# Small triangular inverses moved from two engines to one, and a softplus written with fewer operations, in a two-layer hybrid encoder

## The chip, the cores and the metric

The kernel runs on one core of a Trainium2 chip. The metric is the time of one execution on the device, in microseconds (us); the number to beat is the median of three runs. The profile is of one more execution. The engines are named as the profile names them: PE is TensorE's matrix products, PEld its weight loads, DVE is VectorE, ACT ScalarE, POOL GpSimd, SP SyncE, which here only issues DMAs.

## The reference

Two layers of an encoder over 256 tokens of 1024 channels, in float32. In each layer one projection of the normalised input feeds two token mixers, retention and a gated delta rule in both directions, and two gates. The delta rule is done in chunks of 128 tokens, 8 heads, and needs two things that matter here: a decay g from a softplus, and the inverse of a unit triangular matrix of 128 x 128 for each chunk, head and direction.

```python
h = rmsnorm(x, norm1_g[l])
(r_q, r_k, r_v, r_g, d_q, d_k, d_v, d_z, d_b, d_a, gate_raw) = split_cols(h @ w_in[l])
o = retention_bidir(rotary(r_q), rotary(r_k), r_v)           # then group norm, silu(r_g)
qkv = silu(centred_dwconv(concat([d_q, d_k, d_v]), conv_w[l]))   # 5 taps
beta = sigmoid(d_b)
g = -exp(a_log[l]) * softplus(d_a + dt_bias[l])
od = gated_delta_chunked(...) forward + the same on the flipped sequence
x = x + (gA * (y_ret @ w_proj_ret[l]) + gB * (y_dn @ w_proj_dn[l])) @ w_out[l]
x = x + square(relu(rmsnorm(x) @ w_ff1[l])) @ w_ff2[l]

# inside gated_delta_chunked, per chunk:
gc = cumsum(g)
a_mat = beta[..., :, None] * (kc @ kc.T) * exp(gc_i - gc_j) below the diagonal
sol = triangular_solve(a_mat + eye(CHUNK), rhs, lower=True, unit_diagonal=True)
```

## The kernel before

**Weights and products.** Every weight streams in once, in chunks of 512 KB, by DMAs that SP issues (lines L187 and L205; the tiles are wraw and wrawc, three buffers). ACT copies a chunk to a rounded tile whi (L177), and DVE subtracts that from the original to get the rest, wlo (L178); so a float32 product becomes three products with 32-bit rounded operands. whi and wlo have three buffers each. tok_chunk (L194 to L196) makes 12 products of 512 columns from a chunk, chan_pair (L212 to L214) 24 products of 256 columns. Loads and splits are given a priority that puts them 45 steps ahead of their products (WPRI).

**A layer** has these parts, in the order of the code. Norm 1 and the transposed input. Then gates_small: a small projection, softplus on it (L283 to L308), the product with triangles of ones for the cumulative decays (ps_gc, L313), their rows to DRAM (rowd, L326) and back, spread over all partitions, as E (L333). POOL subtracts the columns (L336) and keeps one triangle (L340), ACT takes the exponential. Then retention and the delta rule, interleaved; then the gates and output projections (chan_pair over ga, pr, gb, pd), and the feed-forward part, which is long and streams weights only.

**The delta rule** is a generator with these steps, for two halves of four heads each:

- half_inputs: for each pair of heads conv_pair, that is chan_pair, then DVE puts the result in a padded tile (xpad, L363), ACT makes tap 0 into an accumulator cacc (L369), POOL tap 4 into cac for the first 16 heads (L371) and ACT for the others, DVE adds taps 1 to 3 (three operations, L375), POOL adds cac to cacc (L376). ACT then makes Silu of it (kq, L394), and TensorE transposes it (ps_kt, L396).
- delta_kk: products of keys and queries (ps_kk), multiplied on DVE with E. The 32 x 32 diagonal blocks of the triangular matrix A go to DRAM (gd).
- delta_solve, once for both halves: the 128 diagonal blocks come back as one block per partition (Gm, L478, 128 x 1024), and the inverse of each is solved there into X, by rows. Step j subtracts the product of row j of A with column j of X from the part of X right of j; there are 30 steps. A step is a pair of operations: a product into stm (L487) and a subtraction in X (L489). X is first set to -Gm (L481), and its diagonal to 1 (L482). The columns of the inverse do not depend on each other, so two engines share them: DVE solves four, POOL the other 28.
- delta_levels: a transposed copy XT (L491, DVE), both to DRAM (xd L493, xtd L494), and back by 40 small DMAs into the tiles dd, D64 and DT of the two halves; then products build the inverses of blocks of 64 (ps_y, L528; ps_m, L538; ps_mt) and of 128 (ps_y6, ps_m6).
- half_v: the same convolution for the values, Silu (L430) in place, and its transposes (ps_vt, L432); delta_out: the recurrence itself.

The parts of the solve that the change touches:

```python
CV = 4
...
for e, c0, c1 in ((V, 0, CV), (G, CV, 32)):
    e.tensor_scalar(X[:, c0:c1, :], Gm[:, c0:c1, :], -1.0, None, ALU.mult)     # L481
    e.memset(X.rearrange("p a b -> p (a b)")[:, 33 * c0:33 * c1 - 32:33], 1.0)
    for j in range(c0 + 1, 31):
        n, w = 31 - j, min(j, c1) - c0
        ...                      # stm = Gm row j x X column j (L487), X -= stm (L489)
```

**The order.** Retention (0) and the delta rule (1) are interleaved by steps in the order `SEQ = "11111011101101"`. That is the order of the code; a scheduler that simulates the engines with costs of its own then sets the order of the instructions on each engine, with the priorities given. An engine runs its instructions in that order, one after the other; so does SP its DMA issues. An instruction whose input is late holds up all that stand behind it on the same engine. The retention part that lies beside the solve consists of its tok_chunks, its scores (ps_st, L690, times a mask into sT, L692) and outputs (ps_ro, L697).

Of the kernel before, what the change touches and what calls it, by code (L numbers as in the profile page):

```python
# [8 lines left out]
F32 = mybir.dt.float32  # L9
F32R = mybir.dt.float32r  # L10
AF = mybir.ActivationFunctionType
ALU = mybir.AluOpType
AX = mybir.AxisListType

P = 128
# [20 lines left out]
def tile_trunk(ctx, tc, x, norm1_g, w_in, conv_w, a_log, dt_bias, ret_gn_g, dn_norm_g,  # L36
# [18 lines left out]
    # how far ahead of the products their weights are loaded and split  # L55
    WPRI = 45
    WRAW = 3
    # the order of the steps of retention (0) and of the delta rule (1)
    SEQ = "11111011101101"
    # columns of the 32 x 32 inverses that VectorE solves; GpSimd the others  # L60
    CV = 4
    # heads whose last tap of the convolution is GpSimd's
    PT = 16
# [31 lines left out]
    def upper(t, s):  # L95
        """keeps t[p, j] where s (j - p) >= 0"""
        G.affine_select(t, t, pattern=[[s, P]], base=0, channel_multiplier=-s, compare_op=ALU.is_ge, fill=0.0)
# [28 lines left out]
    def parameters():  # L126
        # triangles of ones: i <= j, i >= j
        G.memset(tri, 1.0)
        upper(trif, 1)
        upper(trib, -1)  # L130
        columns(cw[0], crow[0], CK * 24)
        A.activation(nega, nega, AF.Exp)
        V.tensor_scalar(nega, nega, -1.0, None, ALU.mult)
# [10 lines left out]
    def rms(nm, xh):  # L144
        """1 / rms of each token: [P, NT]"""
# [11 lines left out]
    def tsplit(src, scale, dst_hi, dst_lo, nm):  # L157
        """dst[j][:, k, :] (channels on partitions) = scale * src transposed, as a float32r pair"""
# [22 lines left out]
    def tok_chunk(w, hi, lo, nk, nm):  # L181
        """two banks [tokens, 512] = act @ w (nk k-tiles of 128 rows, 512 columns)"""
# [16 lines left out]
    def chan_pair(w, hi, lo, nm):  # L199
        """two banks [128 columns of w, S tokens] for w of 256 columns"""  # L200
# [20 lines left out]
    for l in range(DEPTH):  # L221
# [32 lines left out]
        def gates_small():  # L254
# [12 lines left out]
            with tc.high_priority(offset=300):  # L267
# [14 lines left out]
                # softplus(a + dt) = max(a, 0) + log1p(exp(-|a|))  # L282
                ad = s16("ad")  # L283
                G.tensor_tensor(ad, ab[:, :, 16:32],
                                dtb[:, 16 * l:16 * l + 16].unsqueeze(1).broadcast_to([P, NT, 16]), ALU.add)
                m = s16("spm")
                G.tensor_scalar(m, ad, 0.0, None, ALU.max)
                G.tensor_tensor(y, ad, m, ALU.subtract)
                G.tensor_tensor(y, y, m, ALU.subtract)
                A.activation(by, by, AF.Exp)  # L290
                # beta = 1 / (1 + exp(-b)); z = y / (2 + y)
                z = s16("spz")
                V.tensor_scalar(z, y, 2.0, None, ALU.add)
                V.reciprocal(z, z)
                V.tensor_scalar(beta, beta, 1.0, None, ALU.add)
                V.reciprocal(beta, beta)
                G.tensor_tensor(z, z, y, ALU.mult)
                w2 = s16("spw")
                G.tensor_tensor(w2, z, z, ALU.mult)
                p = s16("spp")  # L300
                G.tensor_scalar(p, w2, 1.0 / 15.0, None, ALU.mult)
                for n in (13, 11, 9, 7, 5, 3, 1):
                    G.tensor_scalar(p, p, 1.0 / n, None, ALU.add)
                    G.tensor_tensor(p, p, w2 if n > 1 else z, ALU.mult)
                G.tensor_scalar(p, p, 2.0, None, ALU.mult)
                G.tensor_tensor(p, p, m, ALU.add)
                g = s16("gg")
                G.tensor_tensor(g, p, nega[:, 16 * l:16 * l + 16].unsqueeze(1).broadcast_to([P, NT, 16]), ALU.mult)  # L308
                # cumulative decays of each chunk, both ways
# [17 lines left out]
            # decays of each pair of tokens, exp(gc_i - gc_j) where i is past j and zero elsewhere  # L327
# [28 lines left out]
        def conv_pair(off, cwoff):  # L356
            """two heads (256 columns): silu(conv(proj)) with channels on partitions, unsilu'd accumulators"""
# [85 lines left out]
        # direction, first and second block of the pairs of blocks that make a block of 64  # L443
        PAIRS = ((0, 0, 1), (0, 2, 3), (1, 1, 0), (1, 3, 2))

        def delta_kk(hf, q):
            """decays, A and attn of a half; the 32 x 32 diagonal blocks of A to DRAM"""
# [27 lines left out]
        def delta_solve():  # L475
            """inverses of the 32 x 32 diagonal blocks, one block per partition"""
# [3 lines left out]
            for e, c0, c1 in ((V, 0, CV), (G, CV, 32)):  # L480
                e.tensor_scalar(X[:, c0:c1, :], Gm[:, c0:c1, :], -1.0, None, ALU.mult)  # L481
                e.memset(X.rearrange("p a b -> p (a b)")[:, 33 * c0:33 * c1 - 32:33], 1.0)  # L482
                for j in range(c0 + 1, 31):
                    n, w = 31 - j, min(j, c1) - c0
                    tm = sm.tile([P, 256 if c0 else 128], F32, tag=f"stm{c0}", name="stm", bufs=1)
                    tv = tm[:, :w * n].rearrange("p (a b) -> p a b", a=w)
                    e.tensor_tensor(tv, Gm[:, j, j + 1:].unsqueeze(1).broadcast_to([P, w, n]),  # L487
                                    X[:, c0:c0 + w, j:j + 1].broadcast_to([P, w, n]), ALU.mult)
                    e.tensor_tensor(X[:, c0:c0 + w, j + 1:], X[:, c0:c0 + w, j + 1:], tv, ALU.subtract)  # L489
# [7 lines left out]
        def delta_levels(hf, q):  # L497
            """transposed inverses of the whole chunks' I + A"""
# [4 lines left out]
            Dv = (xtv, xv)     # rows of D of each direction  # L503
            DTv = (xv, xtv)    # rows of its transpose
# [7 lines left out]
            for b in range(4):  # L512
                # as the first block of a pair, and as the second one
# [11 lines left out]
            # blocks of 64: the pairs of both directions at once  # L525
# [27 lines left out]
            # blocks of 128  # L553
# [373 lines left out]
```

## Time and profile before

| | us |
|---|---|
| three runs | 1134.62, 1137.21, 1139.95 |
| median | 1137.21 |
| span of the profiled execution | 1132.0 |
| TensorE busy in it | 1081.0 (95%) |
| DVE busy | 794.1 (70%) |
| ACT busy | 588.2 (52%) |
| POOL busy | 375.5 (33%) |

The profiled execution is one of its own, whose time is known by its span alone: from the first to the last instruction on the engines, without what the launch adds around it. A line of the profile's windows gives a stretch of time and how long each engine was busy in it; a line of its waits gives an instruction's engine, tile and line, what it waited for, and for how long in all, how often, and at most. A line of the timeline gives start, duration, engine, line and operation, with the output and inputs by the names above, and in square brackets how long the engine had been idle before and who released it. "PEclk" is the clock that TensorE was granted, 1.00 being full speed.

### The profile page before, as it was taken

The page shows a single profiled execution, that of the slowest core. Times are in us where ns is not written, and L with a number is a line of the kernel's source. Part 1 is how long each engine was busy: PE and PEld are TensorE (multiplying, and loading weights), DVE is VectorE, ACT ScalarE, POOL GpSimd, SP SyncE. Part 2 cuts the span into 40 slices and gives each one's busy share as a digit, 9 for nine tenths or more (in the row PEclk, how much of TensorE's full clock was granted, in tenths as well). Part 3 has the DMA queues.
Part 4 walks back from the last instruction along what each step waited for, and adds up shares of the span by engine and source line. Part 5 has one row for each costly group of instructions (what it writes and reads, how often), then busy time and mean ns, then how long its engine had stood idle before and what let it go on. Part 6 is the DMA issues. An engine that isn't in the chain of part 4 may idle for free.

```text
span 1132.0 us, 19926 instructions
## 1 busy us (share of the span) xinstructions
PE 1081.0 (95%) x7572; PEld 999.6 (88%) x7572; DVE 794.1 (70%) x1354; ACT 588.2 (52%) x1012; POOL 375.5 (33%) x431
## 2 busy tenths in 40 slices
PE   7979989899999999999998799899999999999997
PEld 6979877799999899988898798778999999999885
DVE  5889989556766666645478999895657676666453
ACT  5677644343355565544367675444334556655342
POOL 4888486100002043300069972940001011332000
PEclk9999999999999999999999999999999999999999
DMA  7464663543465566556564556455443565655653
GB/s 231 150 181 140 180 189 120 132 149 97 130 185 186 168 192 183 185 190 208 175 203 142 174 158 198 135 165 121 128 139 115 176 212 165 201 181 181 199 188 110
DMA packets 175762, 188.45 MB, mean 166 GB/s; under 512 B 36240, under 2 KB 137010, under 8 KB 175666
## 3 DMA queue, kind: packets, MB, share of 16 engines
q1 hardware_dynamic: 174288, 185.17, 53.1%
q10 hardware_dynamic: 1378, 2.02, 0.6%
q8 instruction: 59, 0.97, 0.4%
q14 instruction: 37, 0.30, 0.1%
HBM read 181.85 MB, written 5.31 MB: 165 GB/s over the span
## 4 chain that ended last, share of the span: by engine, by line
PE 70%; DVE 12%; POOL 7%; DMA 3%; issue 3%; SPq 2%; ACT 2%; POOLq 0%; DVEq 0%; ACTq 0%
PE pcf L212 5%; PE pcf L213 5%; PE pcf L214 5%; PE paf L195 5%; PE paf L196 5%; PE paf L194 5%; DVE wlo L178 4%; DVE cacc L375 2%; POOL cacc L376 1%; POOL X L489 1%; PE pcgb L214 1%; PE pcgb L212 1%; PE pcgb L213 1%; DMA wrawc<-in_w_in_dram 1%; PE pawo L196 1%
## 5 line engine op out<-in xcount | busy, mean ns | idle before, releaser
L178 DVE TENSOR_TENSOR wlo<-wrawc,whi 128x1024 fp32r<-128x1024 f32 x192 | 244.4, 1274 | 119.6 <-ACT whi L177 118.5
L177 ACT ACTIVATE whi<-wrawc 128x1024 fp32r<-128x1024 f32 x192 | 202.4, 1055 | 158.9 <-PE pcpr L213 29.0
L178 DVE TENSOR_TENSOR wlo<-wraw,whi 128x1024 fp32r<-128x1024 f32 x128 | 158.7, 1241 | 101.2 <-ACT whi L177 101.0
L177 ACT ACTIVATE whi<-wraw 128x1024 fp32r<-128x1024 f32 x128 | 135.4, 1058 | 132.7 <-PE paf L196 85.6
L213 PE MATMUL pcf<-h2l,whi 128*128 128x256 f32 x512 | 143.7, 283 | 0.0
L214 PE MATMUL pcf<-h2h,wlo 128*128 128x256 f32 x512 | 143.0, 283 | 0.0
L212 PE MATMUL pcf<-h2h,whi 128*128 128x256 f32 x512 | 142.0, 284 | 0.0
L214 PE MATMUL pcd<-hTh,wlo 128*128 128x256 f32 x384 | 109.6, 292 | 2.4 <-DVE wlo L178 2.4
L212 PE MATMUL pcd<-hTh,whi 128*128 128x256 f32 x384 | 111.1, 293 | 0.4 <-DVE xpad L363 0.2
L213 PE MATMUL pcd<-hTl,whi 128*128 128x256 f32 x384 | 110.7, 290 | 0.0
L848 POOL TENSOR_TENSOR fz<-fz 128x256 f32<-128x256 f32 x64 | 66.1, 1034 | 118.1 <-ACT fz L847 117.1
L195 PE MATMUL paf<-wlo,fh 128*128 128x512 f32 x256 | 100.3, 392 | 0.0
L196 PE MATMUL paf<-whi,fl 128*128 128x512 f32 x256 | 100.0, 391 | 0.0
L213 PEld LDWEIGHTS pcf<-h2l,whi 128*128 128x128 f32 x512 | 98.2, 192 | 0.0
L214 PEld LDWEIGHTS pcf<-h2h,wlo 128*128 128x128 f32 x512 | 98.0, 192 | 0.0
L212 PEld LDWEIGHTS pcf<-h2h,whi 128*128 128x128 f32 x512 | 97.1, 192 | 0.0
L194 PE MATMUL paf<-whi,fh 128*128 128x512 f32 x256 | 89.6, 389 | 0.0
L375 DVE SCALAR_TENSOR_TENSOR cacc<-xpad,cw,cacc 128x256 f32<-128x256 f32 x144 | 83.6, 603 | 5.8 <-ACT cacc L369 5.5
L214 PEld LDWEIGHTS pcd<-hTh,wlo 128*128 128x128 f32 x384 | 73.9, 195 | 3.1 <-DVE wlo L178 2.6
L212 PEld LDWEIGHTS pcd<-hTh,whi 128*128 128x128 f32 x384 | 74.9, 196 | 1.8 <-DVE rw L665 0.6
L213 PEld LDWEIGHTS pcd<-hTl,whi 128*128 128x128 f32 x384 | 75.0, 195 | 0.7 <-issue 0.2
L141 POOL TENSOR_TENSOR odf<-sso,mh 128x8 f32<-128x8 f32 x4 | 6.5, 1637 | 199.6 <-DVE sso L642 199.6
(279 smaller groups left out, 2841.2 us busy)
## 6 DMA issues: line engine op xcount, KB each, us to landing
wrawc<-in_w_in_dram SPq DMA_DIRECT2D x96, 512.0 KB, 3.9
wrawc<-in_w_ff_dram SPq DMA_DIRECT2D x64, 512.0 KB, 3.6
wraw<-in_w_ff_dram SPq DMA_DIRECT2D x64, 512.0 KB, 3.6
wraw<-in_w_in_dram SPq DMA_DIRECT2D x48, 512.0 KB, 3.5
wrawc<-in_w_proj_ret_dram SPq DMA_DIRECT2D x16, 512.0 KB, 3.4
wrawc<-in_w_proj_dn_dram SPq DMA_DIRECT2D x16, 512.0 KB, 3.9
wraw<-in_w_out_dram SPq DMA_DIRECT2D x16, 512.0 KB, 3.7
E<-rowd SPq DMA_DIRECT2D x16, 256.0 KB, 5.8
```

Of the source, the lines that this page charges most:

```text
L177: A.activation(hv, raw, AF.Copy)
L178: V.tensor_tensor(lv, raw, hv.bitcast(F32), ALU.subtract)
L194: T.matmul(ps[t], lhsT=a, rhs=wh[:, kk, :], start=k == 0, stop=False)
L195: T.matmul(ps[t], lhsT=a, rhs=wl[:, kk, :], start=False, stop=False)
L196: T.matmul(ps[t], lhsT=b, rhs=wh[:, kk, :], start=False, stop=k == nk - 1)
L212: T.matmul(ps[i], lhsT=wh[:, kk, c], rhs=a, start=k == 0, stop=False)
L213: T.matmul(ps[i], lhsT=wh[:, kk, c], rhs=b, start=False, stop=False)
L214: T.matmul(ps[i], lhsT=wl[:, kk, c], rhs=a, start=False, stop=k == KT - 1)
L375: V.scalar_tensor_tensor(a, xp[:, k:k + S], wk(k), a, ALU.mult, ALU.add)
L376: G.tensor_tensor(a, a, b, ALU.add)
L489: e.tensor_tensor(X[:, c0:c0 + w, j + 1:], X[:, c0:c0 + w, j + 1:], tv, ALU.subtract)
L848: G.tensor_tensor(z2, z, z, ALU.mult)
```

## The change

It does two things. The solve runs on DVE alone: one negation, one memset of the diagonal, and one pair of operations per step j over all j columns that are not finished, so 30 pairs. And softplus, which was 20 operations on POOL beside a few on DVE and ACT, runs on DVE in 14 more: a multiplication and an addition are joined in one operation each time (scalar_tensor_tensor). The series has the same terms as before. Comments and descriptions are dropped as well, so that line numbers after are two to four lower.

```diff
-                G.tensor_tensor(ad, ab[:, :, 16:32],
+                V.tensor_tensor(ad, ab[:, :, 16:32],
                                 dtb[:, 16 * l:16 * l + 16].unsqueeze(1).broadcast_to([P, NT, 16]), ALU.add)
                 m = s16("spm")
-                G.tensor_scalar(m, ad, 0.0, None, ALU.max)
-                G.tensor_tensor(y, ad, m, ALU.subtract)
-                G.tensor_tensor(y, y, m, ALU.subtract)
+                V.tensor_scalar(m, ad, 0.0, None, ALU.max)
+                V.scalar_tensor_tensor(y, m, -2.0, ad, ALU.mult, ALU.add)
                 A.activation(by, by, AF.Exp)
                 z = s16("spz")
                 V.tensor_scalar(z, y, 2.0, None, ALU.add)
                 V.reciprocal(z, z)
+                V.tensor_tensor(z, z, y, ALU.mult)
+                w2 = s16("spw")
+                V.tensor_tensor(w2, z, z, ALU.mult)
+                p = s16("spp")
+                V.tensor_scalar(p, w2, 1.0 / 15.0, None, ALU.mult)
+                for n in (13, 11, 9, 7, 5, 3):
+                    V.scalar_tensor_tensor(p, p, 1.0 / n, w2, ALU.add, ALU.mult)
+                V.scalar_tensor_tensor(p, p, 1.0, z, ALU.add, ALU.mult)
+                V.scalar_tensor_tensor(p, p, 2.0, m, ALU.mult, ALU.add)
+                g = s16("gg")
+                V.tensor_tensor(g, p, nega[...], ALU.mult)
                 V.tensor_scalar(beta, beta, 1.0, None, ALU.add)
                 V.reciprocal(beta, beta)
-                G.tensor_tensor(z, z, y, ALU.mult)
-                w2 = s16("spw")
-                G.tensor_tensor(w2, z, z, ALU.mult)
-                p = s16("spp")
-                G.tensor_scalar(p, w2, 1.0 / 15.0, None, ALU.mult)
-                for n in (13, 11, 9, 7, 5, 3, 1):
-                    G.tensor_scalar(p, p, 1.0 / n, None, ALU.add)
-                    G.tensor_tensor(p, p, w2 if n > 1 else z, ALU.mult)
-                G.tensor_scalar(p, p, 2.0, None, ALU.mult)
-                G.tensor_tensor(p, p, m, ALU.add)
-                g = s16("gg")
-                G.tensor_tensor(g, p, nega[...], ALU.mult)
...
-            for e, c0, c1 in ((V, 0, CV), (G, CV, 32)):
-                e.tensor_scalar(X[:, c0:c1, :], Gm[:, c0:c1, :], -1.0, None, ALU.mult)
-                e.memset(X.rearrange("p a b -> p (a b)")[:, 33 * c0:33 * c1 - 32:33], 1.0)
-                for j in range(c0 + 1, 31):
-                    n, w = 31 - j, min(j, c1) - c0
-                    tm = sm.tile([P, 256 if c0 else 128], F32, tag=f"stm{c0}", name="stm", bufs=1)
-                    tv = tm[:, :w * n].rearrange("p (a b) -> p a b", a=w)
-                    e.tensor_tensor(tv, Gm[:, j, j + 1:].unsqueeze(1).broadcast_to([P, w, n]),
-                                    X[:, c0:c0 + w, j:j + 1].broadcast_to([P, w, n]), ALU.mult)
-                    e.tensor_tensor(X[:, c0:c0 + w, j + 1:], X[:, c0:c0 + w, j + 1:], tv, ALU.subtract)
+            V.tensor_scalar(X, Gm, -1.0, None, ALU.mult)
+            V.memset(X.rearrange("p a b -> p (a b)")[:, 0:1024:33], 1.0)
+            for j in range(1, 31):
+                n = 31 - j
+                tm = sm.tile([P, 256], F32, tag="stm", name="stm", bufs=1)
+                tv = tm[:, :j * n].rearrange("p (a b) -> p a b", a=j)
+                V.tensor_tensor(tv, Gm[:, j, j + 1:].unsqueeze(1).broadcast_to([P, j, n]),
+                                X[:, :j, j:j + 1].broadcast_to([P, j, n]), ALU.mult)
+                V.tensor_tensor(X[:, :j, j + 1:], X[:, :j, j + 1:], tv, ALU.subtract)
```

The scheduler sets the instructions of the changed kernel in another order in three places that matter.

POOL, from the last convolution add ahead of the solve in layer 0 (each row is a line, an operation, its output, its inputs and the shape). Before:

```order
L376 TENSOR_TENSOR cacc<-cacc,cac_2175 128x256
L481 TENSOR_SCALAR X<-Gm 128x896
L376 TENSOR_TENSOR cacc<-cacc,cac_2184 128x256
L482 MEMSET X 128x28
L487 TENSOR_TENSOR stm<-Gm,X 128x26
L489 TENSOR_TENSOR X<-X,stm 128x26
L487 TENSOR_TENSOR stm<-Gm,X 128x50
L489 TENSOR_TENSOR X<-X,stm 128x2x25
```

After:

```order
L468 COPY W<-A_1329 32x8x32 x2
L468 COPY W<-A_1330 32x8x32 x2
L373 TENSOR_TENSOR cacc<-cacc,cac_2086 128x256
L373 TENSOR_TENSOR cacc<-cacc,cac_2095 128x256
L373 TENSOR_TENSOR cacc<-cacc,cac_2253 128x256
L373 TENSOR_TENSOR cacc<-cacc,cac_2262 128x256
```

Two by two, the convolution adds of the values follow each other on POOL now (L373 is L376 of before), and the 52 solve steps that stood between them are gone from this queue.

SP, from the load of Gm to the first small DMA of the levels (dd) in layer 0. Before:

```order
L478 DMA Gm<-gd 128x1024
L187 DMA wraw<-in_w_in_dram 128x2x512 x4
L205 DMA wrawc<-in_w_in_dram 128x4x256 x2
L187 DMA wraw<-in_w_in_dram 128x2x512 x8
L205 DMA wrawc<-in_w_in_dram 128x4x256 x2
L493 DMA xd<-X 128x1024
L494 DMA xtd<-XT 128x1024
L205 DMA wrawc<-in_w_in_dram 128x4x256
L515 DMA dd<-xd 32x8x32
```

After:

```order
L475 DMA Gm<-gd 128x1024
L185 DMA wraw<-in_w_in_dram 128x2x512 x2
L203 DMA wrawc<-in_w_in_dram 128x4x256 x2
L185 DMA wraw<-in_w_in_dram 128x2x512 x8
L203 DMA wrawc<-in_w_in_dram 128x4x256 x6
L489 DMA xd<-X 128x1024
L203 DMA wrawc<-in_w_in_dram 128x4x256
L490 DMA xtd<-XT 128x1024
L511 DMA dd<-xd 32x8x32
```

Between the blocks' load and xd stand 18 weight loads now, and 16 before; Gm itself stands two loads later, so xd follows 58 loads of the layer and not 54.

TensorE, at the second half's first level in layer 0. Before, gate products (pcga) and transposes of retention's output (pstyr) stand between ps_y, ps_m and what follows:

```order
L214 MATMUL pcga_3058<-hTh_124,wlo 128x256
L528 MATMUL ps_y<-dd,W 128x32 x8
L538 MATMUL ps_m<-W,DT_1572 32x32 x8
L164 MATMUL pstyr<-ident,rg_2658 128x128 x8
L212 MATMUL pcga_3058<-hTh_124,whi 128x256
```

After:

```order
L212 MATMUL pcga_3167<-hTh_123,wlo 128x256
L524 MATMUL ps_y<-dd,W 128x32 x8
L534 MATMUL ps_m<-W,DT_1483 32x32 x8
L534 MATMUL ps_m<-W,DT_1484 32x32 x8
L534 MATMUL ps_m<-W,DT_1509 32x32 x8
L534 MATMUL ps_m<-W,DT_1510 32x32 x8
L541 MATMUL ps_mt<-dd,W 128x32 x16
L210 MATMUL pcga_3166<-hTh_124,whi 128x256
```

The levels of 64 of both halves stand together now, with no other products among them.

More of the change, by code (lines that the diff above doesn't have):

```diff
@@ L59, in tile_trunk @@
     SEQ = "11111011101101"
-    CV = 4
     PT = 16
@@ L294, in gates_small @@
                 V.reciprocal(z, z)
+                V.tensor_tensor(z, z, y, ALU.mult)
[8 more added lines that the diff above has]
+                g = s16("gg")
+                V.tensor_tensor(g, p, nega[:, 16 * l:16 * l + 16].unsqueeze(1).broadcast_to([P, NT, 16]), ALU.mult)
                 V.tensor_scalar(beta, beta, 1.0, None, ALU.add)
                 V.reciprocal(beta, beta)
-                G.tensor_tensor(z, z, y, ALU.mult)
-                w2 = s16("spw")
-                G.tensor_tensor(w2, z, z, ALU.mult)
-                p = s16("spp")
-                G.tensor_scalar(p, w2, 1.0 / 15.0, None, ALU.mult)
-                for n in (13, 11, 9, 7, 5, 3, 1):
-                    G.tensor_scalar(p, p, 1.0 / n, None, ALU.add)
-                    G.tensor_tensor(p, p, w2 if n > 1 else z, ALU.mult)
-                G.tensor_scalar(p, p, 2.0, None, ALU.mult)
-                G.tensor_tensor(p, p, m, ALU.add)
-                g = s16("gg")
-                G.tensor_tensor(g, p, nega[:, 16 * l:16 * l + 16].unsqueeze(1).broadcast_to([P, NT, 16]), ALU.mult)
                 g2 = g.rearrange("p t u -> p (t u)")
```

## The prediction

> **What bounds the kernel now.** I read the page's head first, then a table of windows (each row: the window, its length, then busy time and count of TensorE's products, its weight loads, DVE, ACT and POOL, and TensorE's clock), then the waits of each window in which TensorE loses time.
>
> ```profile
> span 1132.0 us, 19926 instructions
> ```
>
> ```profile
> core 0: us, PE busy (x) PEld busy (x) DVE busy (x) ACT busy (x) POOL busy (x), PEclk, DMA share, GB/s
> 20.00:60.00 40.00, 38.20 (x308) 36.99 (x308) 34.03 (x66) 27.90 (x65) 31.92 (x44) 1.00 0.52 157
> 60.00:100.00 40.00, 33.72 (x247) 32.50 (x247) 37.30 (x56) 29.14 (x58) 38.65 (x28) 0.91 0.54 162
> 146.00:206.00 60.00, 54.88 (x284) 47.10 (x283) 54.08 (x124) 27.02 (x40) 42.92 (x63) 0.97 0.51 163
> 260.00:570.00 310.00, 310.00 (x2144) 287.89 (x2143) 190.66 (x266) 151.62 (x230) 44.98 (x45) 1.00 0.55 174
> 620.00:660.00 40.00, 32.07 (x244) 31.11 (x245) 37.29 (x55) 27.29 (x59) 35.86 (x27) 0.96 0.55 168
> 705.00:765.00 60.00, 53.91 (x277) 46.02 (x276) 53.06 (x124) 26.32 (x39) 42.01 (x63) 0.97 0.49 157
> ```
>
> TensorE sets the time: from 260 to 570 us it is never idle at clock 1.00, and nothing of the change lies there. It idles only in the mixer's front, at the same places of both layers: the gates and their decay matrices (20 to 100, 580 to 660), the small inverses (146 to 206, 705 to 765) and the levels built on them, which follow. The change can gain only what is lost there: 27 us of idle TensorE in the five rows (1.8, 6.3, 5.1, 7.9 and 6.1), 2.6 and 1.7 at the levels (below), and what a clock under 1.00 costs.
>
> **The profiled run** has a span of 1132.0 us; the three timed runs lie 5.2 us above it in the median (1137.2). I work in microseconds of the profiled run and add the sum to 1137.2.
>
> **Part 1, the inverses: POOL's queue.** The chain at the first stall, in order of time:
>
> ```profile
> 160.55 1.07 DVE L375 SCALAR_TENSOR_TENSOR cacc<-xpad,cw,cacc 128x256 f32<-128x256 f32 x2
> 162.04 1.50 POOL L487 TENSOR_TENSOR stm<-Gm,X 128x162 f32<-128x162 f32 x1
> 165.22 0.72 POOL L376 TENSOR_TENSOR cacc<-cacc,cac 128x256 f32<-128x256 f32 x1
> 165.97 0.42 ACT L430 ACTIVATE cacc<-cacc 128x256 f32<-128x256 f32 x1 [5.26 <-POOL cacc L376]
> 166.44 0.69 PE L432 MATMUL ps_vt<-ident,cacc 128*128 128x128 f32 x2 [2.90 <-ACT cacc L430]
> 166.00:170.00 4.00, 3.56 (x13) 3.20 (x14) 2.57 (x4) 3.74 (x6) 3.77 (x6) 0.57 0.09 23
> ```
>
> The convolution's accumulator is ready on DVE at 161.6, but the last add (L376) stands in POOL's queue behind solve steps until 165.2. ACT waits 5.26 us, TensorE 2.90, and then runs 4 us at a clock of 0.57. In layer 1:
>
> ```profile
> PE ps_vt L432 <- ACT cacc L430: 3.9, 1, 3.9
> PE parg L195 <- DVE wlo L178: 1.4, 1, 1.4
> PE ps_st L690 <- DVE sT L692: 0.8, 1, 0.8
> 726.00:730.00 4.00, 4.00 (x19) 3.65 (x19) 3.16 (x5) 3.11 (x5) 3.69 (x6) 0.57 0.21 49
> ```
>
> Without solve steps on POOL, the add runs when DVE delivers. Gone: 2.9 + 3.9 of waiting and, at clock 0.57 for 4 us twice, 2 x 4 x 0.43 = 3.4. Term a: -10.2. The 1.4 and 0.8 are DVE's and ACT's, and stay.
>
> By the Trainium skill (TensorE: Matmul & The Clock Gate, Part 1, HAM oscillation) only TensorE gaps over about 3.4 us cost the clock; this trace has 0.57 after a gap of 2.90. By the rule the first stall would not have cost its 1.7 us, and the sum below would be 1.7 us higher; I follow the row.
>
> **Part 1, the inverses: DVE's load.** 28 of the 32 columns, 26 pairs of steps on POOL, now go to DVE.
>
> ```profile
> 147.78 0.18 DVE L487 TENSOR_TENSOR stm<-Gm,X 128x30 f32<-128x30 f32 x1
> 148.22 0.22 DVE L487 TENSOR_TENSOR stm<-Gm,X 128x58 f32<-128x58 f32 x1
> 148.73 0.24 DVE L487 TENSOR_TENSOR stm<-Gm,X 128x84 f32<-128x84 f32 x1
> 163.68 0.53 DVE L487 TENSOR_TENSOR stm<-Gm,X 128x84 f32<-128x84 f32 x1
> L489 DVE TENSOR_TENSOR X<-X,stm 128x84 f32<-128x84 f32 (+28 forms) x30 | 10.5, 350 | 0.4
> L487 DVE TENSOR_TENSOR stm<-Gm,X 128x84 f32<-128x84 f32 (+28 forms) x30 | 10.0, 334 | 0.6
> ```
>
> From 30 elements (0.18) to 84 (0.24) an operation costs 0.143 us and 1.15 ns an element. From start to start it is 0.255 (148.22 to 148.73, with one L489 between), 0.035 to 0.045 more than the record's 0.22. The same 84 elements took 0.53 at 163.68, in the middle of POOL's two-input steps (162.04 is one); at 148 POOL ran its one-input negation. I take the quick price, since POOL's steps are what goes. The changed solve has 60 operations as before; step j has j(31 - j) elements, 4960 over all j, twice: 9920. That is 60 x 0.188 + 9920 x 0.00115 = 11.3 + 11.4 = 22.7 us, 0.38 an operation. The bounds are 0.34 (the two groups' mean, for 56 elements on average) and 0.60 (0.53 at 84 elements, and 0.07 more for the 165 that a step has on average).
>
> Other work on DVE in 146 to 206 was 54.08 - 20.5 = 33.6 us, with 17 weight splits; in the order after, 17 stand between the negation and the transposed copy (13 before). So DVE needs 33.6 + 22.7 + 0.2 (a negation of 1024 elements and not 128) = 56.5 us. TensorE's work for it:
>
> ```profile
> 410.00:470.00 60.00, 60.00 (x503) 60.00 (x502) 37.51 (x41) 35.64 (x64) 21.68 (x21) 1.00 0.60 185
> 490.00:560.00 70.00, 70.00 (x311) 57.41 (x310) 34.17 (x32) 29.36 (x33) 0.96 (x1) 1.00 0.60 198
> 179.74 2.75 PE L697 MATMUL ps_ro<-rv,sT 128*128 128x256 f32 x12
> ```
>
> A product of 256 columns takes 60 / 503 = 0.119 us, of 512 columns 70 / 311 = 0.225. The 17 chunks are 11 of 12 wide products and 6 of 24 narrow ones: 11 x 2.70 + 6 x 2.86 = 46.9. Beside them stand 48 products of retention at 2.75 / 12 = 0.23 (11.0) and eight transposes (two in 0.69 at half clock; 1.3). Sum 59. TensorE still bounds, by 2.5 us of 59. So near to full, a queue in order makes its neighbour wait now and then: I charge 1.0 us a layer, between 0 and the 1.4 + 0.8 of today a second time. Term e: +2.0.
>
> **Part 2, softplus.** POOL's 20 small operations become 14 more on DVE.
>
> ```profile
> PE ps_kt L396 <- ACT kq L394: 1.7, 3, 0.9
> PE ps_gc L313 <- POOL gg L308: 1.5, 1, 1.5
> PE ps_kt L396 <- ACT kq L394: 5.0, 5, 1.4
> L303 POOL TENSOR_SCALAR spp<-spp 128x32 f32<-128x32 f32 x7 | 3.8, 541 | 0.6
> 30.10 0.17 DVE L293 TENSOR_SCALAR spz<-by 128x32 f32<-128x32 f32 x1
> 30.19 0.17 DVE L295 TENSOR_SCALAR by<-by 128x32 f32<-128x32 f32 x1
> ```
>
> The first two rows are layer 0 (20 to 70), the third layer 1 (580 to 636). ps_gc's 1.5 goes: the chain costs 0.54 a step on POOL and 0.17 on DVE, and the products now stand after 14.0 chunks, not 10.3. ps_kt waits for Silu, Silu for POOL's add, behind those 20 small ones; other POOL work (decay matrices, last taps) stays in that queue, so I take two thirds of 6.7: 4.5. Against that, 14 operations a layer at 0.17 at most on a DVE that is 85% busy here: 28 x 0.17 = 4.8, of which records that start 0.09 apart and idle gaps hide some 60%: +1.9. Term b: -1.5 - 4.5 + 1.9 = -4.1; bounds 0 and -8.2 (all the waits gone, DVE free).
>
> **Part 3, the decay matrices** (60 to 100, 620 to 660) stay on POOL, but their DMAs stand after 19 weight loads and not 16, as the row of cumulative decays does (19, not 15).
>
> ```profile
> 75.29 5.04 DVE L375 SCALAR_TENSOR_TENSOR cacc<-xpad,cw,cacc 128x256 f32<-128x256 f32 x3
> 74.44 2.69 POOL L336 TENSOR_TENSOR E<-E,gx 128x1024 f32<-128x1024 f32 x1
> PE pcrq L214 <- DVE wlo L178: 4.9, 3, 3.8
> ```
>
> Three DVE operations of 0.55 took 5.04 while POOL subtracted; the split behind them came late, and TensorE waited. The pair of engines meets here after the change too. POOL, rid of softplus, has its backlog shorter when E arrives, so I take a little, -2; bounds -8 (half of the 14 us that the two rows idle) and +6 (E three chunks later and kk waiting).
>
> **Part 4, the levels.** SP first sends X and its transposed copy, then 40 small DMAs that hold back every weight load behind them:
>
> ```profile
> 199.62 0.34 SPq L493 DMA_DIRECT2D xd<-X  x1
> 225.18 9.87 SPq L205 DMA_DIRECT2D wrawc<-in_w_in_dram  x5
> PE ps_y L528 <- DMA dd<-xd: 2.6, 1, 2.6
> PE ps_y L528 <- DMA dd<-xd: 1.7, 1, 1.7
> ```
>
> So TensorE lives on split chunks from 199.6 to 225. In the order after, xd follows 58 loads (54 before; layer 1: 219, 214), and ps_y stands after 56.9 and 59.0 chunks (51.8 and 53.6). Between the transposed copy and the block TensorE has three chunks left in layer 0, four in layer 1 (four in both before), and 16 products of ps_ro (3.7 us) have moved ahead of the copy. At worst this adds 2.8 + 3.7 = 6.5 and 3.7, 10.2 in all; nothing, if TensorE arrives late by its full three buffers. Since DVE has only 2.5 us in hand, TensorE lags little: term d +6.
>
> Work that stands later now (POOL's convolution adds, transposes of vt) is covered by the split chunks. XT comes 5 chunks later, so fewer gate chunks remain after the last outputs: about 17 us, 35 before, and still enough.
>
> **Sum.** -10.2 + 2.0 - 4.1 - 2 + 6 = -8.3: 1137.2 - 8.3 = 1128.9, say 1129.
>
> **Rivals.**
> DVE becomes the bound of the inverses (slower). For it: a neck of 2.5 us, and rows of 0.53 at 84 elements. Against: 0.24 for the same with POOL on other work. DVE equals TensorE at (59 - 33.8) / 60 = 0.42 an operation. At 0.60 it needs 69.8, 10.8 more in each layer, in place of term e: -10.2 + 21.6 - 4.1 - 2 + 6 = +11.3, so 1148.5. It decides the sign from 0.55. The Trainium skill (VectorE: DVE Perf Modes, The DRAIN you can't avoid) has the next operation wait until the pipe is empty; here 30.19 starts before 30.10 has ended. By the rule, durations add up without overlap.
> Gain eaten (same): half of the ps_vt stall was DVE's (accumulators late behind the solve), a -5; b -2, c 0, d +6: 1136.
> Gain larger: DVE quick once POOL is still, so its own waits of 1.4 and 0.8 go too (a -14.6), b -6, c -6, d 0: 1137.2 - 26.6 = 1110.6.
>
> **Chances.** Forecast 0.50, its own range 1121 to 1134; eaten 0.22; larger 0.12; DVE bound 0.16. No change is what lies within 0.5%, 5.7 us, 1131.5 to 1142.9, about what three runs that spread over 5.3 us can tell. The forecast's upper part, 0.09, lies in it too, as does 0.02 of the DVE case: faster 0.53, same 0.33, slower 0.14. The range leaves out most of the larger gain (0.09) and the DVE case's upper half (0.08): 1113 to 1147.
>
> **What would show it.** No ps_vt wait at L430 and no clock under 1 in the two windows (a). DVE solve operations at 0.33 us in record, 0.38 from start to start, PE waiting for wlo less than 2 us there (e). No ps_gc wait, ps_kt under 2 us (b). Idle of TensorE in the decay stage still above 8 us in all (c). The ps_y waits at 5 us or more in each layer (d). A DVE with no gap between the negation and the copy, and PE waiting for wlo by 10 us, proves me wrong.

## The result, and the profile after

The changed kernel takes 1118.55 us in the median (1117.67 to 1119.09), the kernel before on the same chip 1135.91. The ratio is 0.9858, with an interval of 0.9826 to 0.9891; a second comparison gave 0.9842 (0.9822 to 0.9863). So it is 16 to 18 us faster, where 8 were forecast; 1129 was the number, and 1118.6 lies in the range of 1113 to 1147.

The head of the page after, and the windows of the same stages as before (same columns: TensorE's products, weight loads, DVE, ACT, POOL, TensorE's clock). The two rows with 206:260 and 765:820 are of the kernel before, for the levels.

```profile
span 1116.4 us, 19786 instructions
PE 1081.2 (97%) x7572; PEld 1003.5 (90%) x7572; DVE 789.3 (71%) x1384; ACT 589.2 (53%) x1012; POOL 293.6 (26%) x275
```

```profile
core 0: us, PE busy (x) PEld busy (x) DVE busy (x) ACT busy (x) POOL busy (x), PEclk, DMA share, GB/s
20.00:60.00 40.00, 40.00 (x334) 39.65 (x333) 38.78 (x79) 30.92 (x71) 23.87 (x20) 1.00 0.58 165
60.00:100.00 40.00, 33.17 (x259) 31.67 (x259) 36.05 (x62) 29.68 (x63) 37.44 (x29) 0.98 0.57 173
146.00:206.00 60.00, 60.00 (x336) 52.87 (x335) 55.65 (x137) 30.66 (x45) 8.62 (x8) 1.00 0.61 179
206.00:250.00 44.00, 42.20 (x385) 41.40 (x385) 23.09 (x40) 18.41 (x35) 1.91 (x2) 0.84 0.56 143
700.00:760.00 60.00, 59.60 (x338) 52.63 (x337) 57.83 (x141) 31.40 (x49) 8.76 (x8) 1.00 0.56 165
760.00:805.00 45.00, 43.12 (x394) 41.96 (x393) 20.55 (x35) 15.92 (x28) 1.91 (x2) 0.81 0.51 128
```

```profile
206.00:260.00 54.00, 50.65 (x482) 47.93 (x481) 29.16 (x56) 22.70 (x40) 1.59 (x3) 0.94 0.44 114
765.00:820.00 55.00, 52.91 (x513) 50.13 (x512) 32.79 (x61) 22.67 (x40) 2.13 (x3) 0.97 0.46 119
```

In the solve's window TensorE is busy for all 60.00 us at clock 1.00, with 336 products and not 284. DVE is busy for 55.65, hardly more than the 54.08 of before, though it does the whole solve now. In the levels the clock has become worse, 0.84 and 0.81.

A table by stage says where the 16 us are. For each kind of product I take the 25th percentile of its distance from start to start over all these traces as its undisturbed length, and add up what each product took beyond that: TensorE's lost time, idle gaps and slow clock together. The front reaches from 20 us (in layer 1: 575) to the negation that starts the solve, the solve from there to the transposed copy, the levels are the 45 us after it. The numbers are both layers' sums in us; the rows from e1 on are the experiments below. A second profile of the changed kernel (e11) gave 33.6, 5.9, 18.4 and 10.4, which tells how well such numbers repeat. e10 has no row: its trace is of one of its longest runs (below).

| run | front | solve | levels | rest of the mixer and feed-forward | ratio to before, interval |
|---|---|---|---|---|---|
| before | 37.8 | 20.0 | 16.3 | 10.0 | |
| after | 33.2 | 5.4 | 19.1 | 10.3 | 0.9858 (0.9826 to 0.9891) |
| e1: solve alone | 36.8 | 5.0 | 23.8 | 10.5 | 0.9938 (0.9917 to 0.9960) |
| e2: softplus alone | 33.8 | 17.4 | 17.5 | 11.1 | 0.9964 (0.9943 to 0.9984) |
| e3: before, no add in POOL's queue | 37.2 | 18.3 | 13.1 | 10.4 | 0.9973 (0.9956 to 0.9990) |
| e4: after, products doubled | 37.1 | 5.3 | 23.8 | 27.6 | 1.0099 (1.0074 to 1.0124) |
| e5: after, no add on POOL | 31.9 | 4.9 | 21.3 | 10.0 | 0.9868 (0.9847 to 0.9889) |
| e6: e5 and POOL kept busy | 32.7 | 18.2 | 20.6 | 9.6 | 0.9975 (0.9961 to 0.9988) |
| e7: after, 20 small DMAs on ACT | 32.8 | 5.7 | 14.0 | 10.2 | 0.9818 (0.9794 to 0.9842) |
| e8: after, 20 small DMAs on POOL | 33.3 | 6.4 | 11.0 | 25.6 | 0.9908 (0.9878 to 0.9938) |
| e9: after, decays subtracted on ACT | 34.6 | 5.2 | 16.1 | 17.9 | 0.9923 (0.9902 to 0.9944) |
| e12: after, all 40 small DMAs on ACT | 33.9 | 5.4 | 32.4 | 10.9 | 0.9995 (0.9978 to 1.0011) |

The solve gained 14.6 us, the front 4.6, and the levels gave 2.8 back. The two groups of DVE's solve operations after, in layer 0:

```profile
L485 DVE TENSOR_TENSOR X<-X,stm 128x30 f32<-128x30 f32 (+14 forms) x30 | 10.2, 340 | 0.4
L483 DVE TENSOR_TENSOR stm<-Gm,X 128x30 f32<-128x30 f32 (+14 forms) x30 | 10.2, 340 | 0.4
```

Sixty operations on 9920 elements take 20.4 us. Before, sixty on a third of the elements took 20.5. The solve on DVE cost nothing, because each operation had been slowed as much as it has grown. That is the thread that the experiments follow.

### The profile page after: what moved, and what is told of

Read it like the earlier page. It is cut to its first block, busy times and chain, and to the rows that moved or that the text cites. A ratio compares the mean times of both kernels' runs of the same rounds, so it can differ in the third digit from the quotient of the medians.

```text
span 1116.4 us, 19786 instructions
## 1 busy us (share of the span) xinstructions
PE 1081.2 (97%) x7572; PEld 1003.5 (90%) x7572; DVE 789.3 (71%) x1384; ACT 589.2 (53%) x1012; POOL 293.6 (26%) x275
## 4 chain that ended last, share of the span: by engine, by line
PE 69%; DVE 12%; DMA 6%; issue 5%; POOL 4%; SPq 3%; ACT 2%; POOLq 0%; ACTq 0%; DVEq 0%
PE pcf L210 6%; PE pcf L212 6%; PE pcf L211 6%; PE paf L194 5%; PE paf L193 5%; PE paf L192 5%; DVE wlo L176 3%; DVE cacc L372 3%; DMA wrawc<-in_w_in_dram 2%; PE pcpr L211 1%; PE pcpr L210 1%; PE pcpr L212 1%; PE pcgb L210 1%; PE pcgb L212 1%; PE pcgb L211 1%
## 5 line engine op out<-in xcount | busy, mean ns | idle before, releaser
L373 POOL TENSOR_TENSOR cacc<-cacc,cac 128x256 f32<-128x256 f32 x48 | 49.9, 1048 | 96.2 <-DVE cacc L372 72.3
```

The costliest lines, as they stand in the source:

```text
L373: G.tensor_tensor(a, a, b, ALU.add)
```

## The experiments

**e1 and e2: each part alone.** e1 is the kernel before with the new solve, as the change has it; e2 is the changed kernel with the old split:

```diff
+    CV = 4
-            V.tensor_scalar(X, Gm, -1.0, None, ALU.mult)
...
+            for e, c0, c1 in ((V, 0, CV), (G, CV, 32)):
+                e.tensor_scalar(X[:, c0:c1, :], Gm[:, c0:c1, :], -1.0, None, ALU.mult)
...
```

> Only the solve is changed; softplus stays on POOL as before. Queue theory (the solve leaving POOL's queue is the cause): the solve stages lose some 15 us less TensorE time, as the changed kernel's two stages did (9.8 to 2.4 and 11.0 to 3.1), and the levels give back up to 4: 11 to 15 us under the kernel before. Rival (softplus and the decay stage carry the gain, the solve's part is given back at the levels): not more than 5 us under it.

> Only softplus is changed; the solve stays split between DVE (4 columns) and POOL (28). Queue theory: the wait of the vt transposes for POOL's add stays (2.9 and 3.9 us before), and only the front stages gain, 3 to 6 us. Rival (softplus carries it): 10 us or more. Second rival (softplus gains nothing, later decays eat it): within 2 us.

The solve alone gives 0.6%, 7 us; softplus alone 0.4%, 4 us. In the table the solve's 15 us are all there in e1 (20.0 to 5.0), as both stages' windows show, but the levels take 7.5 of them back:

```profile
146.00:206.00 60.00, 60.00 (x336) 52.87 (x335) 57.57 (x139) 31.79 (x47) 10.86 (x10) 1.00 0.61 180
206.00:260.00 54.00, 50.09 (x461) 48.56 (x461) 25.38 (x44) 19.16 (x36) 0.95 (x1) 0.81 0.42 104
```

That is more than expected (up to 4), and so the total missed the 11 to 15. e2's time came as expected: 4 us in the front, and the solve stage still loses 17.4. But the wait that was expected to stay did not. ps_vt waits for 1.0 us in layer 0, where it waited for 2.9, and not at all in layer 1, where it waited for 3.9; TensorE waits for DVE's splits and masks in its place. The waits of e2 in the solve, layer 0 and then layer 1:

```profile
PE parg L194 <- DVE wlo L177: 3.5, 2, 2.5
PE ps_st L688 <- DVE X L487: 1.7, 1, 1.7
PE ps_vt L430 <- ACT cacc L428: 1.0, 1, 1.0
PE ps_st L688 <- DVE sT L690: 2.5, 1, 2.5
PE parg L194 <- DVE wlo L177: 1.5, 1, 1.5
```

So the add's place in POOL's queue is only one of the places where this stage's loss can show. The two parts together give some 5 us more than the sum of each alone, hardly more than the intervals allow, and in the table that lies in the levels of layer 0 (13.1 in e1, 8.7 after). The scheduler orders those levels differently in each kernel; which difference of order it is was not isolated.

**e3: the queue taken away, the split solve left.** This is the kernel before; the values' last tap, so far ACT's, becomes a fourth DVE operation, so that no add stands in POOL's queue behind the solve:

```diff
                 if cstate["n"] <= PT:
                     G.tensor_scalar(b, xp[:, 4:4 + S], wk(4), None, ALU.mult)
+                    for k in (1, 2, 3):
+                        V.scalar_tensor_tensor(a, xp[:, k:k + S], wk(k), a, ALU.mult, ALU.add)
+                    G.tensor_tensor(a, a, b, ALU.add)
                 else:
-                    A.activation(b, xp[:, 4:4 + S], AF.Copy, scale=wk(4))
-                for k in (1, 2, 3):
-                    V.scalar_tensor_tensor(a, xp[:, k:k + S], wk(k), a, ALU.mult, ALU.add)
-                G.tensor_tensor(a, a, b, ALU.add)
+                    for k in (1, 2, 3, 4):
+                        V.scalar_tensor_tensor(a, xp[:, k:k + S], wk(k), a, ALU.mult, ALU.add)
```

> The kernel before with one edit: the last tap of the values' convolution is a fourth operation on DVE, and POOL's add behind it is gone, in both layers. Solve and softplus as before, so POOL and DVE still run two-input operations side by side. Queue alone as the cause: no wait of vt for POOL, 10 us under the kernel before. Sharing between POOL and DVE as the cause: DVE's solve operations still take 0.35 us at 56 elements on average, TensorE waits for DVE's splits instead, and less than 5 us is gained.

It gained 0.3%, 3 us, and the solve stage still lost 18.3 of 20.0. The wait of ps_vt for POOL is gone, and others stand in its place. From the waits of TensorE in the two solve windows (what it waited for, sum, times, longest), then from the timeline:

```profile
PE ps_st L691 <- DVE stm L488: 3.0, 1, 3.0
PE parg L195 <- DVE wlo L178: 3.6, 3, 2.0
PE ps_st L691 <- DVE X L490: 3.0, 1, 3.0
```

```profile
169.47 0.58 DVE L488 TENSOR_TENSOR stm<-Gm,X 128x84 f32<-128x84 f32 x1
170.03 0.51 POOL L488 TENSOR_TENSOR stm<-Gm,X 128x180 f32<-128x180 f32 x1
170.09 0.56 DVE L490 TENSOR_TENSOR X<-X,stm 128x84 f32<-128x84 f32 x1
171.23 0.23 DVE L488 TENSOR_TENSOR stm<-Gm,X 128x80 f32<-128x80 f32 x1
```

84 elements take DVE 0.56 to 0.58 us beside POOL's steps, and 80 take 0.23 where the operation started between two of them. The edit gives DVE 8 more operations a layer (some 4 us), which weighs on the same queue, and takes 8 from ACT; so e3 shows that taking away POOL's queue is not enough, not how the 18.3 divide.

**e5 and e6: the sharing alone.** e5 is the changed kernel with the edit of e3. e6 adds to that 38 two-input operations a layer on POOL at the time of the solve, whose result nobody reads. Every other engine, SP's DMAs included, runs the same instructions in the same order in both:

```diff
+            c2 = cc[:, :1024].rearrange("p (a b) -> p a b", a=32)
+            tm2 = sm.tile([P, 192], F32, tag="stm2", name="stm2", bufs=1)
+            G.tensor_scalar(tm2, Gm.rearrange("p a b -> p (a b)")[:, :192], -1.0, None, ALU.mult)
+            for j in range(5, 24):
+                n, w = 31 - j, j - 4
...
+                tv2 = tm2[:, :w * n].rearrange("p (a b) -> p a b", a=w)
+                G.tensor_tensor(tv2, c2[:, j, j + 1:].unsqueeze(1).broadcast_to([P, w, n]),
+                                c2[:, 4:4 + w, j:j + 1].broadcast_to([P, w, n]), ALU.mult)
+                G.tensor_tensor(tv2, tv2, c2[:, 4:4 + w, j + 1:], ALU.subtract)
```

> The changed kernel with the values' last tap as a fourth DVE operation and no add on POOL, the basis for the next run. DVE gets 8 operations a layer of some 0.47 us more, 3.8 us. If DVE were the neck of the solve stage, 3 to 4 us a layer, some 7 over the changed kernel. If the copy only moves behind more splits: within 3 us of it, that is 13 to 18 us under the kernel before.

> The run before this one plus 38 two-input operations on POOL during the solve, in the old shapes, from constants into a scratch tile that nobody reads; nothing that matters waits for them and the other engines' order is the same. Sharing theory (two-input operations of DVE and POOL get in each other's way): DVE's solve operations that lie beside them take 0.5 us and more and not 0.25 to 0.40, TensorE waits for DVE, and the time is 8 to 18 us over e5_after_tap. Rival (only POOL's queue did it): within 2 us of it.

e5 is as fast as the changed kernel (0.9868), although DVE does 4 us more a layer. e6 is 12 us slower than e5 (1131.95 and 1119.82, on the same chip), 12 of the 15 that e5 had gained. Windows over the solve in e5 (153:216) and e6 (152:222), with the same work in both to a few instructions:

```profile
153.00:216.00 63.00, 63.00 (x372) 56.30 (x371) 60.10 (x150) 31.88 (x48) 4.95 (x4) 1.00 0.58 167
```

```profile
152.00:222.00 70.00, 65.83 (x374) 57.70 (x372) 67.10 (x149) 31.73 (x48) 31.31 (x43) 0.98 0.52 150
```

e6's longest wait in the solve of each layer, where e5 has none in either:

```profile
PE parg L193 <- DVE wlo L176: 2.0, 1, 2.0
PE parg L193 <- DVE wlo L176: 3.5, 1, 3.5
```

And one solve operation of 130 elements, from the timelines of e6 and then of the changed kernel:

```profile
164.77 0.50 DVE L497 TENSOR_TENSOR X<-X,stm 128x130 f32<-128x130 f32 x1
```

```profile
161.19 0.29 DVE L485 TENSOR_TENSOR X<-X,stm 128x130 f32<-128x130 f32 x1
```

Nobody reads what those POOL operations write, and what stands behind them on POOL holds DVE up by 0.8 us in layer 0 in both runs. (Once a layer the profile names one of them as what ended a wait of a weight load for ps_st; that load reads nothing of theirs, and TensorE's products waited for DVE's sT there.) So this is no queue: DVE's two-input operations are slowed by POOL's. DVE's busy time grows by 7 us, the stage by 7, and TensorE's lost time rises from 4.9 to 18.2, the sum of both layers. As the order is the same, the operations can be compared one by one. Of the 7 us in layer 0, 4.3 lie on the 60 solve steps, 1.3 on the splits and 1.2 on the accumulations; the rest did not change. 20 of the 60 steps lie beside one of the added operations, and 17 of these take 1.6 to 2.0 times as long as in e5; the 40 others differ by 2% at most.

**e4: is DVE the neck of the solve?** The changed kernel, with the solve's products done twice:

```diff
                 V.tensor_tensor(tv, Gm[:, j, j + 1:].unsqueeze(1).broadcast_to([P, j, n]),
                                 X[:, :j, j:j + 1].broadcast_to([P, j, n]), ALU.mult)
+                V.tensor_tensor(tv, Gm[:, j, j + 1:].unsqueeze(1).broadcast_to([P, j, n]),
+                                X[:, :j, j:j + 1].broadcast_to([P, j, n]), ALU.mult)
```

> The changed kernel with each of the solve's 30 products done twice: 30 x 0.34 = 10.2 us more of DVE work a layer, in the same stage. If DVE is the neck there with 2.5 us in hand, as forecast, TensorE waits 7 to 8 us more in each layer: some 15 us over the changed kernel. Rival (the copy of the inverses only moves behind more weight splits, and TensorE has other work for that time): less than 5 us over it.

Both theories missed: it is 25 us slower than the changed kernel by the medians, 27 by the ratios, but not in the solve. There TensorE is never idle; 17 of the 25 us come 50 us and more after it, the rest in the front and the levels. Windows of the solve in layer 0, and of the time in which the mixer ends:

```profile
154.00:241.00 87.00, 87.00 (x567) 79.83 (x566) 82.60 (x196) 45.74 (x69) 8.68 (x8) 1.00 0.57 166
290.00:360.00 70.00, 65.22 (x555) 62.30 (x555) 43.71 (x100) 25.81 (x42) 3.27 (x2) 0.98 0.31 95
```

The scheduler put 27 splits and not 17 between the negation and the copy, so TensorE had work all through the longer solve. It used up the gate chunks with which it would have filled the recurrence behind the levels: the last ps_o stood behind 80 chunks of the layer and not 74, and 80 are all there are before the next input is needed. Most of the price of a longer solve is paid there, 17 us of "rest" in the table; the 4 in the front and 5 in the levels were not followed up.

**e7, e8 and e12: the levels' small DMAs.** The changed kernel, with the second half's 20 small DMAs issued by ACT (e7), by POOL (e8), or all 40 by ACT (e12):

```diff
-                DQ.dma_start(...)          # each of those in delta_levels
+                (DQ if hf == 0 else nc.scalar).dma_start(...)     # e7
+                (DQ if hf == 0 else G).dma_start(...)             # e8
+                nc.scalar.dma_start(...)                          # e12
```

> The changed kernel with the second half's 20 small DMAs of the levels issued by ACT and not by SP. If the two levels stages lose their 8.5 and 10.8 us of TensorE because SP's 40 small DMAs hold back weight loads, loads start 10 us earlier and 5 to 10 us are gained over the changed kernel: ratio to the kernel before near 0.98. If they lose it in the chain of the levels' own small products: within 2 us of the changed kernel. If ACT's weight roundings wait behind its DMAs: slower than it.

> The same 20 DMAs issued by POOL, which has 2 us of work in the levels stage. SP's block theory: a gain of 5 to 10 us over the changed kernel, as with ACT but with no rounding held up. Rival: the last products of the mixer now stand behind all but one of the gate chunks that fill the time, and TensorE waits there: 3 us or more slower than the changed kernel.

> All 40 small DMAs of the levels on ACT, where e7_dma_act had 20. If SP's block is what costs the levels, another 2 to 5 us under e7_dma_act: ratio to the kernel before 0.977 to 0.980. If ACT's roundings of the weights, which stand behind the DMAs in ACT's queue, take the place of the held-back loads: as slow as the changed kernel or slower, 0.984 and up.

e7 takes 1113.57 us, ratio 0.9818; the changed kernel's two ratios are 0.9858 and 0.9842. It is the fastest version here by its median, 3 to 5 us under the changed kernel by ratio, though the intervals overlap. The levels lose 14.0 and not 19.1, and the clock in them is better:

```profile
206.00:250.00 44.00, 41.59 (x404) 40.69 (x404) 25.64 (x43) 19.31 (x37) 1.91 (x2) 0.92 0.58 152
760.00:805.00 45.00, 42.21 (x432) 40.58 (x430) 21.93 (x35) 15.95 (x29) 0.52 (x1) 0.89 0.49 126
```

e8 brings the levels down to 11.0, the best of all, and loses 15 us at the mixer's end, as its rival said: the last products of the mixer stand behind all gate chunks there, as in e4. e12 loses all the gain. ACT issued 40 DMAs one behind the other, some waiting for their data, and rounded no weights for that time; the waits of ACT and of TensorE in layer 0's levels:

```profile
ACT W L529 <- DMA DT<-xtd: 22.2, 1, 22.2
PE ps_y L524 <- DMA dd<-xd: 7.0, 1, 7.0
PE ps_m L534 <- DVE W L527: 3.2, 1, 3.2
```

So TensorE loses 5 to 8 us less in the levels when half of SP's block stands in another queue. That it is the block alone is argued, not shown: the scheduler also set another order on TensorE, DVE and ACT in each of these kernels. The whole of it, moved to an engine that TensorE needs, costs more than it did on SP.

**e9 (and e10): the same sharing in the decay stage.** In the changed kernel an accumulation takes 2.15 us and not 0.47 beside one of POOL's subtractions from E. e9 leaves these out on POOL and has ACT subtract by the bias of its exponential:

```diff
+                ngc = s16("ngc")
+                V.tensor_scalar(ngc, gc, -1.0, None, ALU.mult)
...
-                    G.tensor_tensor(E, E, gc[:, :, i0:i0 + HH].unsqueeze(3).broadcast_to([P, NT, HH, P]),
-                                    ALU.subtract)
...
-                A.activation(Es[hf], Es[hf], AF.Exp)
...
+                            A.activation(Es[hf][:, d, c, h, :], Es[hf][:, d, c, h, :], AF.Exp,
+                                         bias=ngc[:, c, i:i + 1])
```

> The changed kernel without POOL's four two-input subtractions of 1024 elements a layer in the decay stage: ACT subtracts in its exponential, by a bias, in 32 operations of 128 elements and not 2 of 2048. Sharing theory: single DVE operations that lie beside those subtractions (an accumulation of 2.15 us and not 0.47 at 73.8, splits of 1.75, 2.09 and 2.25 us and not 1.22) come back to their usual length, and of the front stages' 33 us of lost TensorE time 4 to 10 go. Rival (the front loses its time in the chain of Silu and transposes on a busy ACT, which gets more to do here): no gain, or slower.

> The same together with the second half's small DMAs of the levels on ACT: if the two act in different stages, the gains add, 5 us more than the first alone, ratio to the kernel before near 0.975.

e9 is slower than the changed kernel (0.9923), by its rival. ACT's 32 exponentials cost 9.7 us for the two that cost 3.8, and TensorE waits for ACT's rounding:

```profile
L348 ACT ACTIVATE E<-E,ngc 128x128 f32<-128x128 f32 x32 | 9.7, 390 | 0.2 <-POOL E L337 0.2
PE pcrq L210 <- ACT whi L175: 3.3, 1, 3.3
```

The accumulation of 2.15 us is gone, but DVE's operations did not all come back to their length: POOL still selects the triangle from E there, an operation with one input, and an accumulation beside it takes 1.09 us and not 0.47.

```profile
73.25 1.10 POOL L337 TENSOR_SCALAR_AFFINE_SELECT E<-E 128x1024 f32<-128x1024 f32 x1 [2.93 <-DMA E<-rowd]
73.53 1.09 DVE L377 SCALAR_TENSOR_TENSOR cacc<-xpad,cw,cacc 128x256 f32<-128x256 f32 x1
```

The front lost 34.6, 33.2 before the edit, so e9 does not tell what the sharing costs in the decay stage; some 8 us more are lost late in the mixer, and their cause stays open. e10, the same with e7's DMAs, gained nothing clear beyond it: 0.9951 (0.9917 to 0.9984), where 0.975 was expected. Its twelve runs lie between 1122.6 and 1138.8 us and its trace is of one of 1137.2, so what happened there stays open; e7's gain did not add.

> The changed kernel once more, on the same chip as the two above: between 15 and 19 us under the kernel before, ratio 0.983 to 0.989, as measured first.

That was the changed kernel again: 1117.49 us, ratio 0.9842 (0.9822 to 0.9863).

## Why the prediction was right, and where its sizes were off

- **What bounds the kernel**: right. TensorE sets the time, and all of the gain lies in the three stages named (14.6, 4.6, and -2.8). The direction was right too, but the gain is twice the forecast, and the largest term was right in its sign by a mechanism that is only in part the one at work: that is partly luck.
- **Term a, the waits of ps_vt**: the waits and the half clock behind them went, and with them the 1.4 and 0.8 that I had left standing as DVE's own: 14.6 in all, where I had 10.2. The mechanism was only half right. I put the stall down to the add's place in POOL's queue. e3 takes that away, with 8 more DVE operations a layer, and the stage gains 1.7 us; in e2 most of the ps_vt wait is gone with the solve still split, and the stage loses 17.4; e6 has nothing that matters in POOL's queue, lets POOL run beside DVE, and the stage loses 13.3 more than in e5. The 0.53 against 0.24 for 84 elements, which I quoted for the price of a solve step, was the main cause itself, and it slows splits and accumulations as well.
- **DVE's load**: 0.33 an operation in the record was forecast, and 0.34 came; 56.5 us were forecast for the stretch from the negation to the end of the copy, and it took 56.3 (150.4 to 206.7). The 0.38 from start to start holds where one step follows the other directly (0.40); where another operation of DVE stands between, that one starts before the step's record has ended, and over all steps it is 0.31. **Term e**, +2.0 for a queue that is nearly full, was 0. e4 shows why: with 10 us more DVE work the solve stage still loses 5.3. The copy moves behind more splits, and TensorE has those to work on. A and e together: -8.2 forecast, -14.6 measured; this is the term that was mis-sized, and 6.4 of the 8 us by which the stages' sum (-16.4) misses the forecast.
- **Terms b and c, the front**: -6.1 forecast, -4.6 measured (e2 alone: -4.0). The wait of ps_gc is gone. ps_kt waits for 1.7 us and not 5.0 in layer 1, but for 3.0 and not 1.7 in layer 0. TensorE still idles in the decay stage (6.8 us in the window 60:100 above, 6.3 before), as expected, with POOL's subtractions in it. Softplus, with the addition ahead of it and the product behind it, is 24 operations on POOL in the trace of before, and 15 more on DVE in that of after, where the text ahead of the prediction and term b say 20 and 14; at the 0.17 us that term b charges, this would move it by 0.1.
- **Term d, the levels**: +6 forecast, +2.8 measured, by another way than I said. The waits of ps_y did not grow: there is none in layer 0, and 1.4 in layer 1. TensorE is idle there for 1.8 and 1.9 us, not more than before (3.4 and 2.1), and loses the rest in the half clock that follows short gaps (clock 0.84 and 0.81). The waits in layer 0:

```profile
PE ps_m L534 <- DMA DT<-xtd: 0.9, 1, 0.9
PE ps_m L534 <- DVE D L536: 0.5, 1, 0.5
PE ps_m L534 <- DVE W L527: 0.4, 1, 0.4
```

- **The rivals**: "DVE becomes the bound" is out, by the 0.34 of the groups and by e4. "Gain larger" had the right mechanism in its first term, -14.6, DVE quick once POOL is still; its other terms did not come. I gave it 0.12, too little for what the two rows of 84 elements already showed. Two slips in the rivals' arithmetic change none of this: 81 more elements at 1.15 ns add 0.09 and not 0.07 to the 0.53, and by the prediction's own sum the sign turns at 0.51 an operation; 0.55 is where the loss reaches the 5.7 us that were called no change.

## What to carry to other kernels

Work that is split over two engines is worth it only if the two do not slow each other. Compare the same instruction at the same size with the neighbour busy and idle: where it takes twice as long beside the neighbour, giving all of the work to one engine can cost nothing. When a stage is made shorter or longer, look at where TensorE's filling work runs out later, since that is where the time shows; and before small DMAs are moved off a crowded queue, look at what else stands in the new one.

## What the runs showed of the hardware that was not expected

- **DVE and POOL**: a DVE operation with two inputs in SBUF can take about twice as long beside two-input operations of POOL: 0.56 to 0.58 us and not 0.24 for 84 elements, 0.50 and not 0.29 for 130. Not each one is slowed that much (17 of the 20 steps beside POOL's in e6's layer 0). POOL's operation need not have two inputs (the accumulation of 1.09 us in e9), though POOL's one-input negation left DVE's steps at their quick price (0.24 at 148.73 in the prediction). An accumulation on DVE that started with one of POOL's subtractions of 1024 elements took 2.15 us and not 0.47. The two rows, of the changed kernel:

```profile
73.73 1.90 POOL L333 TENSOR_TENSOR E<-E,gx 128x1024 f32<-128x1024 f32 x1 [2.20 <-DMA E<-rowd]
73.76 2.15 DVE L372 SCALAR_TENSOR_TENSOR cacc<-xpad,cw,cacc 128x256 f32<-128x256 f32 x1
```

The Trainium skill (SBUF — State Buffer, Who interferes with whom) says that DVE's second input goes by a path that it shares with GpSimd, and that one blocks the other. The trace agrees: DVE's operation ends only 0.28 us after POOL's, and operations with one input in PSUM did not change; two masks of the scores, in the changed kernel and in e6 beside POOL's steps:

```profile
166.98 0.74 DVE L688 TENSOR_TENSOR sT<-ps_st,cc 128x256 f32<-128x256 f32 x2
```

```profile
166.33 0.74 DVE L700 TENSOR_TENSOR sT<-ps_st,cc 128x256 f32<-128x256 f32 x2
```

- **The clock**: TensorE's clock fell to half without a long gap. In the levels of layer 0 after, its longest idle time was 0.91 us, yet in the 4 us from 226 it had work for only 2.20, and the clock fell to 0.50 within them and stayed there until about 242:

```profile
226.00:230.00 4.00, 2.20 (x50) 0.78 0.45 64
230.00:234.00 4.00, 4.00 (x29) 0.50 1.01 300
```

(Columns here: TensorE busy, its clock, DMA share, GB/s.) By the Trainium skill (TensorE: Matmul & The Clock Gate, HAM oscillation) idle gaps of over about 3.4 us are what costs the clock; here it also fell after several short ones within 4 us, and waits of 0.4 to 0.9 us were followed by some 13 us at half speed. Whether it was the gaps alone, or also the small products between them (128x32), no run shows.
